# Two places for working buffers: the last 14 of 48 stand 64 bytes further on, and the operands that meet the weights take the others

## The chip, the cores and the metric

The kernel runs on one core of one Trainium2 chip. The metric is device time in microseconds, the time of one launch; the kernel was timed in three runs. One further execution was taken with the hardware profiler, and all rows below come from that one.

## The reference

The reference is a decoder trunk of two layers on 256 tokens of width 1024, all in float32. A layer has four sub-layers, each with its own RMS norm and added to the residual `h`:

```python
for l in range(DEPTH):
    h = h + 0.5 * swiglu_ffn(rms_norm(h, norm_g[l, 0]), ffn_w_in[l, 0], ffn_w_out[l, 0])
    u = rms_norm(h, norm_g[l, 1])
    z = u @ mix_w_in[l]
    ...
    y_a = rwkv7_time_mix(z_a, ...)
    y_b = retention_mix(z_b, positions, b_gn[l])
    ...
    merged = gate_a * (y_a @ w_branch_a[l]) + gate_b * (y_b @ w_branch_b[l])
    h = h + merged @ mix_w_out[l]
    h = h + memory_cross_attn(rms_norm(h, norm_g[l, 2]), mem, mem_norm[l],
                              cross_w_q[l], cross_w_kv[l], cross_w_o[l])
    h = h + 0.5 * swiglu_ffn(rms_norm(h, norm_g[l, 3]), ffn_w_in[l, 1], ffn_w_out[l, 1])
return rms_norm(h, final_norm)
```

The FFN's hidden width is 2816. The mix has an RWKV-7 branch (8 heads of 64) and a retention branch (8 heads, keys of 64, values of 128); the cross attention has 4 heads of 256 over 256 memory tokens.

## The kernel before, in words

The residual is kept transposed (`hT`, feature by token). Every large product is computed as three products of fp32r operands: each operand is split into a high and a low part, and high·high, high·low and low·high are added up in PSUM (`mm3`, which calls `mm` three times). In the profile a product reads "output<-moving,stationary 128\*128 128x256": the stationary operand is 128 by 128, the moving one 128 by 256. In the FFN `uh`/`ul` (the normed input) move and `wh`/`wl` (the weights) are loaded; in the cross attention the scores `xs` have `kT` moving and `qT` loaded, the outputs `xo` have `pT` moving and `xv` loaded, and neither operand is a weight there.

Weights come by DMA on SyncE's queue in pieces of 512 KB into five `raw` buffers; ScalarE makes the high part (`wh`, line 244), VectorE the low part (`wl`, line 245). Each has seven buffers.

Everything else that a stage needs lies in an arena of 49 buffers of 128 partitions by 2 KB (`Slots`, `s.ar`). A tile takes the buffer at the head of a queue of free ones and gives it back to the queue's end. The tiles that share a buffer are tied in order by the framework: who writes the new one waits for the last reader of the old one. Between the weights' pools and the arena stands a tile `pad` of 64 bytes (`PAD = 16` floats), and the pool `up` with `uh` and `ul` comes behind it too. The weight buffers and the arena's buffers are all multiples of 128 bytes long, so `uh`, `ul` and every arena buffer begin 64 bytes away from the 128-byte grid on which `wh` and `wl` begin. In the cross attention's `xs` and `xo` products both operands come from the arena.

The order of TensorE's instructions is written out by an event loop at build time (`Em`): tasks with a priority and a due time in a rough model of TensorE's time. The order on ScalarE, VectorE, GpSimd and SyncE is left to the framework's scheduler, which looks at dependences, at the buffers' reuse among them, and at a priority.

The names that come up below: `S` (line 1149, `mask_evac`) is the evacuation with a mask of the scores of the RWKV-7 branch from PSUM, which the next scores and the chain of that branch need. `yb<-O` (line 1483) normalises the outputs of retention with `brn`, a power that GpSimd computes (line 268) from `bss` (lines 1010 and 1480); `yb<-yb,bg` (line 1495) multiplies by the gate `bg` (lines 1438, 1440). `yaT` is the transposed output of the RWKV-7 branch, `ybT` that of retention, `mT` the merged one. `up`, `uph`, `upl` are the small up-projections of the RWKV-7 branch and their split parts. `rb`, `diagh`, `diagl`, `rx` and `sq` belong to the RMS norms. GpSimd also runs a solver of small triangular systems (`tm`, `xs`, `us`, lines 1188 and 1193).

Of the kernel before, what the change touches and what calls it, by code (L numbers as in the profile page):

```python
# [10 lines left out]
F32 = mybir.dt.float32  # L11
# [5 lines left out]
P = 128  # L17
# [55 lines left out]
class Event:  # L73
    def __init__(s):
        s.t = math.inf
# [40 lines left out]


class Slots:
    def __init__(s, pool, n, prefix, shape):
        s.pool, s.prefix, s.shape = pool, prefix, shape  # L120
        s.free_ = deque(range(n))
        s.used = {}
        s.low = n
        s.names = {}

    def alloc(s, name, dtype=F32, shape=None):
        assert s.free_, (s.prefix, "exhausted", sorted(x[1] for x in s.used.values()))
        i = s.free_.popleft()
        s.low = min(s.low, len(s.free_))
        t = s.pool.tile(list(shape or s.shape), dtype, name=name, tag=f"{s.prefix}{i}")  # L130
        s.used[id(t)] = (i, name, t)
        return t
# [7 lines left out]
class Weights:  # L140
# [10 lines left out]
    def next(s, key):  # L151
        assert s.seq[s.taken][0] == key, (s.seq[s.taken][0], key)
        s.fill()
        t = s.tiles.pop(s.taken)
        s.taken += 1
        return t
# [6 lines left out]
class K:  # L163
    NW = 7
    NRAW = 5
    NA = 49
    T_XG = 57000.0

    def __init__(s, ctx, tc, A):
        s.tc, s.nc, s.A = tc, tc.nc, A  # L170
        nc = s.nc
        ep = ctx.enter_context
        s.em = Em()
        s.pows = []
        s.const = ep(tc.tile_pool(name="const", bufs=1))
        s.rawp = ep(tc.tile_pool(name="raw", bufs=s.NRAW))
        s.wp = ep(tc.tile_pool(name="wp", bufs=s.NW))
        s.sm = ep(tc.tile_pool(name="sm", bufs=2))
        pad = ep(tc.tile_pool(name="pad", bufs=1))
        s.up = ep(tc.tile_pool(name="up", bufs=1))  # L180
        pad.tile([P, PAD], F32, name="pad")
        s.dram = ep(tc.tile_pool(name="dram", bufs=1, space=bass.MemoryType.DRAM))
        s.ar = Slots(ep(tc.tile_pool(name="ar", bufs=1)), s.NA, "a", (P, 512))
        s.ps = Slots(ep(tc.tile_pool(name="ps", bufs=1, space=bass.MemoryType.PSUM)), 8, "p", (P, 512))
        s.W = Weights(s, s.NW)
        s.setup()
        c = s.const
        s.hT = c.tile([P, 8, 256], F32, name="hT")
        s.gcol = c.tile([P, 112], F32, name="gcol")
        nc.scalar.dma_start(s.gcol, A["gcol"])  # L190
        nc.sync.dma_start(s.hT[:, 0:2, :], A["xT"][:, 0:2, :])
        s.ident = c.tile([P, P], F32, name="ident")
        nc.gpsimd.dma_start(s.ident, A["ident"])
        s.cols = c.tile([P, 8], F32, name="cols")
        nc.gpsimd.dma_start(s.cols, A["cols"])
        s.nhalf = c.tile([P, 8], F32, name="nhalf")
        nc.gpsimd.memset(s.nhalf, -0.5)
        s.ones = c.tile([P, P], F32, name="ones")
        nc.gpsimd.memset(s.ones, 1.0)
        s.onesr = c.tile([P, P], F32R, name="onesr")  # L200
        nc.gpsimd.tensor_copy(s.onesr, s.ones)
        s.cumr = c.tile([P, P], F32R, name="cumr")
        s.masks = c.tile([P, 2, P], I32, name="masks")
        s.gam = c.tile([P, 2, 2, 8], F32, name="gam")
        s.rot = [c.tile([P, 64], F32, name=f"rot{t}") for t in range(2)]
        s.S0 = c.tile([P, 4, P], F32, name="S0")
# [1566 lines left out]
```

## Time and profile before

| | us |
|---|---|
| median of 3 runs | 1493.65 |
| lowest and highest of the 3 | 1493.39, 1495.62 |
| the profiled execution's own time | 1494.51 |
| its span in the trace | 1492.7 |
| TensorE busy | 1471.5 |
| VectorE busy | 1062.8 |
| ScalarE busy | 761.4 |
| GpSimd busy | 153.6 |
| DMA moved | 270.54 MB |

The span runs from the first to the last instruction of the trace. The mean granted TensorE clock of the profiled execution is 0.993 of full speed. [...] Idle time in brackets is the time in which an engine waited, with the instruction that released it.

### The profile page before, as it was taken

The page shows a single profiled execution, that of the slowest core. Times are in us where ns is not written, and L with a number is a line of the kernel's source. Part 1 is how long each engine was busy: PE and PEld are TensorE (multiplying, and loading weights), DVE is VectorE, ACT ScalarE, POOL GpSimd, SP SyncE. Part 2 cuts the span into 40 slices and gives each one's busy share as a digit, 9 for nine tenths or more (in the row PEclk, how much of TensorE's full clock was granted, in tenths as well). Part 3 has the DMA queues.
Part 4 walks back from the last instruction along what each step waited for, and adds up shares of the span by engine and source line. Part 5 has one row for each costly group of instructions (what it writes and reads, how often), then busy time and mean ns, then how long its engine had stood idle before and what let it go on. Part 6 is the DMA issues. An engine that isn't in the chain of part 4 may idle for free.

```text
span 1492.7 us, 28682 instructions
## 1 busy us (share of the span) xinstructions
PE 1471.5 (99%) x11776; PEld 1400.1 (94%) x11776; DVE 1062.8 (71%) x1472; ACT 761.4 (51%) x1048; POOL 153.6 (10%) x231
## 2 busy tenths in 40 slices
PE   9999999998999999999999999999899999999998
PEld 9999988888999999999999999887799999999997
DVE  7975699977567757656685667899666567675654
ACT  7554475553445655444464445655354456554442
POOL 2210011281000000000001000204700000000000
PEclk9999999999999999999999999999989999999999
DMA  9776655535446545666577665675355455466661
GB/s 315 225 242 197 186 180 195 170 126 175 155 143 194 172 141 174 202 193 196 170 219 241 192 194 154 196 236 172 87 178 159 155 170 184 127 207 191 196 195 45
DMA packets 137818, 270.54 MB, mean 181 GB/s; under 512 B 18820, under 2 KB 29460, under 8 KB 137688
## 3 DMA queue, kind: packets, MB, share of 16 engines
q1 hardware_dynamic: 134552, 260.99, 56.2%
q0 software_dynamic: 2704, 7.15, 1.7%
q8 instruction: 92, 1.51, 0.4%
q10 hardware_dynamic: 432, 0.58, 0.1%
q14 instruction: 38, 0.31, 0.1%
HBM read 263.31 MB, written 2.23 MB: 178 GB/s over the span
## 4 chain that ended last, share of the span: by engine, by line
PE 87%; POOL 5%; DVE 4%; issue 2%; DMA 2%; SPq 0%; ACT 0%; POOLq 0%; DVEq 0%
PE z L210 25%; PE acc L210 21%; PE u L210 16%; PE g L210 16%; PE xq L210 3%; POOL tm L1188 3%; POOL xs L1193 2%; DVE wl L245 1%; PE tp L222 1%; PE Y L210 1%; PE xo L210 1%; PE xs L210 1%; PE sc L210 1%; PE SA L210 1%; PE low L210 1%
## 5 line engine op out<-in xcount | busy, mean ns | idle before, releaser
L245 DVE TENSOR_TENSOR wl<-raw,wh 128x1024 fp32r<-128x1024 f32 (+1 forms) x478 | 581.6, 1225 | 313.5 <-ACT wh L244 312.3
L244 ACT ACTIVATE wh<-raw 128x1024 fp32r<-128x1024 f32 (+1 forms) x478 | 502.0, 1056 | 504.6 <-PE z L210 150.1
L210 PE MATMUL g<-uh,wl 128*128 128x256 f32 x704 | 195.0, 277 | 0.2
L210 PE MATMUL u<-uh,wh 128*128 128x256 f32 x704 | 195.0, 277 | 0.0
L210 PE MATMUL g<-uh,wh 128*128 128x256 f32 x704 | 194.8, 277 | 0.0
L210 PE MATMUL g<-ul,wh 128*128 128x256 f32 x704 | 194.8, 277 | 0.0
L210 PE MATMUL u<-ul,wh 128*128 128x256 f32 x704 | 194.7, 277 | 0.0
L210 PE MATMUL u<-uh,wl 128*128 128x256 f32 x704 | 194.7, 277 | 0.0
L210 PE MATMUL acc<-ah,wh 128*128 128x256 f32 x528 | 145.8, 276 | 0.0
L210 PE MATMUL acc<-ah,wl 128*128 128x256 f32 x528 | 145.7, 276 | 0.0
L210 PE MATMUL acc<-al,wh 128*128 128x256 f32 x528 | 145.7, 276 | 0.0
L210 PEld LDWEIGHTS g<-uh,wl 128*128 128x128 f32 x704 | 132.2, 188 | 0.6 <-DVE wl L245 0.6
L210 PEld LDWEIGHTS g<-uh,wh 128*128 128x128 f32 x704 | 132.4, 188 | 0.2
L210 PEld LDWEIGHTS g<-ul,wh 128*128 128x128 f32 x704 | 132.2, 188 | 0.2
L210 PEld LDWEIGHTS u<-uh,wl 128*128 128x128 f32 x704 | 132.3, 188 | 0.0
L210 PEld LDWEIGHTS u<-uh,wh 128*128 128x128 f32 x704 | 132.2, 188 | 0.0
L210 PEld LDWEIGHTS u<-ul,wh 128*128 128x128 f32 x704 | 132.2, 188 | 0.0
L210 PE MATMUL z<-wh,uh 128*128 128x512 f32 (+1 forms) x320 | 125.3, 391 | 0.0
L210 PE MATMUL z<-wh,ul 128*128 128x512 f32 (+1 forms) x320 | 122.4, 383 | 0.7 <-DVE ul L436 0.7
L210 PE MATMUL z<-wl,uh 128*128 128x512 f32 (+1 forms) x320 | 121.5, 380 | 0.0
L210 PEld LDWEIGHTS acc<-ah,wh 128*128 128x128 f32 x528 | 99.1, 188 | 0.0
L210 PEld LDWEIGHTS acc<-al,wh 128*128 128x128 f32 x528 | 99.1, 188 | 0.0
(409 smaller groups left out, 3305.3 us busy)
## 6 DMA issues: line engine op xcount, KB each, us to landing
raw<-in_ffn_w_in SPq DMA_DIRECT2D x174, 512.0 KB, 4.5
raw<-in_mix_w_in SPq DMA_DIRECT2D x108, 512.0 KB, 4.4
raw<-in_ffn_w_out SPq DMA_DIRECT2D x88, 512.0 KB, 4.2
raw<-in_cross_w_kv SPq DMA_DIRECT2D x32, 512.0 KB, 3.7
raw<-in_w_branch_b SPq DMA_DIRECT2D x16, 512.0 KB, 3.6
raw<-in_mix_w_out SPq DMA_DIRECT2D x16, 512.0 KB, 3.4
raw<-in_cross_w_q SPq DMA_DIRECT2D x16, 512.0 KB, 3.8
raw<-in_cross_w_o SPq DMA_DIRECT2D x16, 512.0 KB, 4.2
```

The source lines that it names most:

```text
L210: s.nc.tensor.matmul(out, l, r, start=start, stop=stop)
L222: s.nc.tensor.transpose(out, src, s.ident)
L244: s.nc.scalar.activation(hi, src, AF.Copy)
L245: s.nc.vector.tensor_tensor(lo, src, hi.bitcast(F32), ALU.subtract)
L1188: i = nc.gpsimd.tensor_tensor(tm[:, 0:nr, 0:w], xc, row, ALU.mult)
L1193: nc.gpsimd.tensor_tensor(xs[:, 0:nr, k + 1:32], xs[:, 0:nr, k + 1:32], tm[:, 0:nr, 0:w], ALU.add)
```

## The change

The arena has 48 buffers in place of 49. All are now allocated at the start in one go, 34 of them, then a tile `space` of 64 bytes, then the last 14. The last 14 therefore begin on the 128-byte grid on which `wh` and `wl` begin, and the first 34 stay 64 bytes away from it. A tile whose name is in `BY_W` (the operands that are multiplied with weights, and `qT`, `pT`, `diag`) takes the first free buffer of the first part in the queue; any other tile takes the first free buffer of the last part; where that part has none, the head of the queue. `kT`, `xv` and all work that isn't an operand are among the others.

```diff
--- before.py
+++ after.py
@@ -116,16 +116,25 @@
 
 
 class Slots:
-    def __init__(s, pool, n, prefix, shape):
+
+
+    def __init__(s, pool, n, prefix, shape, nb=0, names=()):
         s.pool, s.prefix, s.shape = pool, prefix, shape
+        if nb:
+            for i in range(n):
+                if i == n - nb:
+                    pool.tile([P, 16], F32, name="space", tag="space")
+                pool.tile(list(shape), F32, name=f"{prefix}{i}", tag=f"{prefix}{i}")
         s.free_ = deque(range(n))
+        s.na, s.names = n - nb, names
         s.used = {}
         s.low = n
-        s.names = {}
 
     def alloc(s, name, dtype=F32, shape=None):
         assert s.free_, (s.prefix, "exhausted", sorted(x[1] for x in s.used.values()))
-        i = s.free_.popleft()
+        first = name in s.names
+        i = next((i for i in s.free_ if (i < s.na) == first), s.free_[0])
+        s.free_.remove(i)
         s.low = min(s.low, len(s.free_))
         t = s.pool.tile(list(shape or s.shape), dtype, name=name, tag=f"{s.prefix}{i}")
         s.used[id(t)] = (i, name, t)
@@ -163,7 +172,9 @@
 class K:
     NW = 7
     NRAW = 5
-    NA = 49
+    NA, NB = 48, 14
+
+    BY_W = {n + x for n in ("a", "mT", "yaT", "ybT", "mem", "oT", "qT", "pT", "lt", "tw", "diag", "k") for x in "hl"}
     T_XG = 57000.0
 
     def __init__(s, ctx, tc, A):
@@ -180,7 +191,7 @@
         s.up = ep(tc.tile_pool(name="up", bufs=1))
         pad.tile([P, PAD], F32, name="pad")
         s.dram = ep(tc.tile_pool(name="dram", bufs=1, space=bass.MemoryType.DRAM))
-        s.ar = Slots(ep(tc.tile_pool(name="ar", bufs=1)), s.NA, "a", (P, 512))
+        s.ar = Slots(ep(tc.tile_pool(name="ar", bufs=1)), s.NA, "a", (P, 512), s.NB, s.BY_W)
         s.ps = Slots(ep(tc.tile_pool(name="ps", bufs=1, space=bass.MemoryType.PSUM)), 8, "p", (P, 512))
         s.W = Weights(s, s.NW)
         s.setup()
```

TensorE executes the same products in the same order. The data of `uh`, `ul`, `wh`, `wl` stay where they were. Which buffer a tile gets changes almost everywhere, and with it which earlier tile it has to wait for, so that the scheduler puts some instructions of the other engines elsewhere. Two places follow. The number behind a name tells tiles of one name apart, and lines and numbers of the changed kernel are higher by 9 to 11 and by about 49.

VectorE in the mix of layer 0, around the four normalisations `yb<-O` (layer 1 has the same). Before:

```order
L1480 TENSOR_SCALAR bss_3897<-bss_3897 128x4
L1480 TENSOR_SCALAR bss_3910<-bss_3910 128x4
L1495 TENSOR_TENSOR yb_3878<-yb_3878,bg_3791 128x512
L1483 TENSOR_TENSOR yb_3895<-O_3886,brn_3900 128x512
L1483 TENSOR_TENSOR yb_3908<-O_3903,brn_3913 128x512
L1010 TENSOR_REDUCE bss_3927<-yb_3925 128x4
L245 TENSOR_TENSOR wl_3967<-raw_3965,wh_3966 128x1024
L1480 TENSOR_SCALAR bss_3927<-bss_3927 128x4
L1495 TENSOR_TENSOR yb_3895<-yb_3895,bg_3795 128x512
L1483 TENSOR_TENSOR yb_3925<-O_3916,brn_3930 128x512
```

Now:

```order
L1491 TENSOR_SCALAR bss_3946<-bss_3946 128x4
L1021 TENSOR_REDUCE bss_3959<-yb_3957 128x4
L1494 TENSOR_TENSOR yb_3944<-O_3935,brn_3949 128x512
L1491 TENSOR_SCALAR bss_3959<-bss_3959 128x4
L1021 TENSOR_REDUCE bss_3976<-yb_3974 128x4
L1494 TENSOR_TENSOR yb_3957<-O_3952,brn_3962 128x512
L1491 TENSOR_SCALAR bss_3976<-bss_3976 128x4
L1506 TENSOR_TENSOR yb_3927<-yb_3927,bg_3840 128x512
L1494 TENSOR_TENSOR yb_3974<-O_3965,brn_3979 128x512
L256 TENSOR_TENSOR wl_4016<-raw_4014,wh_4015 128x1024
```

The weight split that stood between the third and the fourth `yb<-O` (wl_3967) and the product of the second `yb` with its gate stand behind the fourth now, and the `bss` scalar that the fourth needs stands directly behind the third.

VectorE directly behind, down to the first masked evacuation `S` of this place. Before, behind yb_3925:

```order
L245 TENSOR_TENSOR wl_3989<-raw_3987,wh_3988 128x1024
L1438 SCALAR_TENSOR_TENSOR bg_3993<-bg_3993,z_3799 128x512
L1438 SCALAR_TENSOR_TENSOR bg_3997<-bg_3997,z_3800 128x512
L1440 SCALAR_TENSOR_TENSOR bg_3993<-bg_3993,rhf_2623,gn_3650 128x512
L1440 SCALAR_TENSOR_TENSOR bg_3997<-bg_3997,rhf_2623,gn_3650 128x512
L245 TENSOR_TENSOR wl_4035<-raw_4033,wh_4034 128x1024
L1495 TENSOR_TENSOR yb_3908<-yb_3908,bg_3993 128x512
L1495 TENSOR_TENSOR yb_3925<-yb_3925,bg_3997 128x512
L245 TENSOR_TENSOR wl_4065<-raw_4063,wh_4064 128x1024
L245 TENSOR_TENSOR wl_4125<-raw_4123,wh_4124 128x1024
L1149 TENSOR_TENSOR S_4103<-sc_4093,masks_97 128x512
```

Now, behind wl_4016:

```order
L1449 SCALAR_TENSOR_TENSOR bg_4042<-bg_4042,z_3848 128x512
L256 TENSOR_TENSOR wl_4038<-raw_4036,wh_4037 128x1024
L1451 SCALAR_TENSOR_TENSOR bg_4042<-bg_4042,rhf_2672,gn_3699 128x512
L1449 SCALAR_TENSOR_TENSOR bg_4046<-bg_4046,z_3849 128x512
L1506 TENSOR_TENSOR yb_3944<-yb_3944,bg_3844 128x512
L1451 SCALAR_TENSOR_TENSOR bg_4046<-bg_4046,rhf_2672,gn_3699 128x512
L256 TENSOR_TENSOR wl_4084<-raw_4082,wh_4083 128x1024
L1506 TENSOR_TENSOR yb_3957<-yb_3957,bg_4042 128x512
L1506 TENSOR_TENSOR yb_3974<-yb_3974,bg_4046 128x512
L256 TENSOR_TENSOR wl_4114<-raw_4112,wh_4113 128x1024
L256 TENSOR_TENSOR wl_4174<-raw_4172,wh_4173 128x1024
L1160 TENSOR_TENSOR S_4152<-sc_4142,masks_146 128x512
```

Between the fourth `yb<-O` and `S` stood four weight splits, four `bg` and two `yb` products before; now there are five, four and three.

VectorE at the head of the mix of layer 1, where the last `ul` parts of the norm are made. Before:

```order
L691 TENSOR_TENSOR hT_82<-hT_82,dh_11128 128x512
L436 SCALAR_TENSOR_TENSOR ul_11002<-hT_82,gcol_83,uh_11001 128x256
L245 TENSOR_TENSOR wl_11147<-raw_11145,wh_11146 128x1024
L436 SCALAR_TENSOR_TENSOR ul_11002<-hT_82,gcol_83,uh_11001 128x256 x2
L446 TENSOR_TENSOR sq_11034<-sq_11034,sq_11135 128x512
L245 TENSOR_TENSOR wl_11153<-raw_11151,wh_11152 128x1024
L449 TENSOR_TENSOR sq_11034<-sq_11034 128x256
```

Now:

```order
L702 TENSOR_TENSOR hT_131<-hT_131,dh_11177 128x512
L447 SCALAR_TENSOR_TENSOR ul_11051<-hT_131,gcol_132,uh_11050 128x256
L256 TENSOR_TENSOR upl_11301<-wup_11290,uph_11298 65x512
L447 SCALAR_TENSOR_TENSOR ul_11051<-hT_131,gcol_132,uh_11050 128x256 x2
L457 TENSOR_TENSOR sq_11083<-sq_11083,sq_11184 128x512
L256 TENSOR_TENSOR upl_11303<-gup_11292,uph_11300 128x512
L460 TENSOR_TENSOR sq_11083<-sq_11083 128x256
```

The three splits `upl` stood some 70 rows further up, in the FFN; now they stand in the norm, and the weight split between the `ul` parts has moved behind them. In layer 0 the three splits moved into the norm too, but there a weight split still stands ahead of the last two `ul` parts.

## Rows read from the trace of the kernel before

**Rows 1.** Two lines of the profile's page: from its first part TensorE's busy time, share of the span and instructions, and from its fourth part the chain that ended last, by engine.

```profile
PE 1471.5 (99%) x11776; PEld 1400.1 (94%) x11776; DVE 1062.8 (71%) x1472; ACT 761.4 (51%) x1048; POOL 153.6 (10%) x231
...
PE 87%; POOL 5%; DVE 4%; issue 2%; DMA 2%; SPq 0%; ACT 0%; POOLq 0%; DVEq 0%
```

**Rows 2.** The list of waits of TensorE over the whole span: who waited for whom, us in total, times, longest.

```profile
PE sc L210 <- DVE S L1149: 11.0, 2, 5.5
```

**Rows 3.** TensorE's instructions in order of time around the second pair of `xo` heads of layer 0: start in us, its modelled duration in us, then engine, line, operation, output<-moving,stationary and count.

```profile
540.62 0.28 PE L210 MATMUL acc<-oTh,wh 128*128 128x256 f32 x1
...
543.68 0.28 PE L210 MATMUL xo<-pTh,xvh 128*128 128x256 f32 x1
...
546.56 0.28 PE L210 MATMUL acc<-oTh,wh 128*128 128x256 f32 x1
...
579.77 0.27 PE L210 MATMUL rb<-ones,sq 128*128 128x128 f32 x1
```

**Rows 4.** Groups of TensorE's instructions, busy us and modelled mean ns of one: first from 540.61 to 543.60 us, then from 546.55 to 579.70 us. Each row stands for one of three products with the same count, mean and operands (hi and lo parts exchanged), give or take one at the edge of the window.

```profile
L210 PE MATMUL acc<-oTh,wh 128*128 128x256 f32 x9 | 2.5, 276 | 0.0
...
L210 PE MATMUL acc<-oTh,wh 128*128 128x256 f32 x54 | 15.2, 281 | 0.0
...
L210 PE MATMUL g<-uh,wh 128*128 128x256 f32 x32 | 9.0, 281 | 0.0
...
L210 PE MATMUL u<-uh,wh 128*128 128x256 f32 x8 | 2.2, 281 | 0.0
```

**Rows 5.** The stretch behind the second pair of `xo` heads in layer 1, its first product and what ends it, in order of time (columns as in rows 3).

```profile
1283.59 0.28 PE L210 MATMUL acc<-oTh,wh 128*128 128x256 f32 x1
...
1316.81 0.27 PE L210 MATMUL rb<-ones,sq 128*128 128x128 f32 x1
```

**Rows 6.** Groups of TensorE's instructions (columns as in rows 4): the first pair of `xo` heads from 530.97 to 533.80 us, and the `xs` products from 511.06 to 513.93 us.

```profile
L210 PE MATMUL xo<-pTh,xvh 128*128 128x256 f32 x8 | 2.3, 283 | 0.0
...
L210 PE MATMUL xs<-kTh,qTh 128*128 128x256 f32 x8 | 2.3, 283 | 0.0
```

**Rows 7.** The products of `yaT` from 465.88 to 474 us as a group (columns as in rows 4), and in order of time the first of the stretch behind them and what ends it (columns as in rows 3).

```profile
L210 PE MATMUL z<-yaTl,wh 128*128 128x256 f32 x24 | 6.6, 276 | 0.0
...
473.94 0.28 PE L210 MATMUL acc<-mTh,wh 128*128 128x256 f32 x1
...
502.50 0.27 PE L210 MATMUL rb<-ones,sq 128*128 128x128 f32 x1
```

**Rows 8.** VectorE in order of time in layer 0, ahead of the evacuation of the masked scores `S` (start, duration of all of the row, line, operation, names, shapes, count, and in brackets idle time before it and its releaser).

```profile
333.76 1.31 DVE L245 TENSOR_TENSOR wl<-raw,wh 128x1024 fp32r<-128x1024 f32 x1
...
335.07 0.68 DVE L1495 TENSOR_TENSOR yb<-yb,bg 128x512 f32<-128x512 f32 x1
336.66 0.69 DVE L1483 TENSOR_TENSOR yb<-O,brn 128x512 f32<-128x512 f32 x1 [0.91 <-POOL brn L268]
337.26 1.22 DVE L245 TENSOR_TENSOR wl<-raw,wh 128x1024 fp32r<-128x1024 f32 x1
338.40 1.28 DVE L1438 SCALAR_TENSOR_TENSOR bg<-bg,z 128x512 f32<-128x512 f32 x2
339.59 1.41 DVE L1440 SCALAR_TENSOR_TENSOR bg<-bg,rhf,gn 128x512 f32<-128x512 f32 x2
340.92 1.22 DVE L245 TENSOR_TENSOR wl<-raw,wh 128x1024 fp32r<-128x1024 f32 x1
342.05 1.29 DVE L1495 TENSOR_TENSOR yb<-yb,bg 128x512 f32<-128x512 f32 x2
343.26 2.35 DVE L245 TENSOR_TENSOR wl<-raw,wh 128x1024 fp32r<-128x1024 f32 x2
345.53 1.28 DVE L1149 TENSOR_TENSOR S<-sc,masks 128x512 int32<-128x512 int32 x2
```

**Rows 9.** GpSimd in the same stretch: the three powers `brn` (columns as in rows 8).

```profile
330.53 2.00 POOL L268 TENSOR_TENSOR brn<-bss,nhalf 128x4 f32<-128x4 f32 x2
...
335.23 1.39 POOL L268 TENSOR_TENSOR brn<-bss,nhalf 128x4 f32<-128x4 f32 x1 [1.24 <-DVE bss L1480]
```

**Rows 10.** TensorE's first product behind the long wait of layer 0, in order of time, and busy time, granted clock (PEclk), DMA share and GB/s in two stretches of each layer: the long wait and what follows it until the clock is back.

```profile
346.27 0.58 PE L210 MATMUL sc<-mh,kh 64*128 64x256 f32 x1 [5.46 <-DVE S L1149]
...
340.65:346.27 5.62, 0.17 (x3) 0.01 (x1) 5.62 (x8) 0.00 (x0) 0.93 (x2) 0.98 0.46 115
346.27:352.85 6.58, 6.56 (x32) 6.04 (x33) 5.88 (x9) 3.76 (x6) 0.00 (x0) 0.50 0.63 168
...
1077.40:1083.08 5.68, 0.18 (x2) 0.00 (x1) 5.68 (x8) 0.00 (x0) 0.99 (x2) 0.72 0.50 122
1083.08:1090.13 7.05, 7.03 (x35) 6.51 (x36) 6.35 (x9) 3.76 (x6) 0.00 (x0) 0.50 0.64 179
```

**Rows 11.** Layer 1 in order of time: the evacuation of `S` on VectorE, and at the head of the mix the last two `ul` tiles with the weight split ahead of them on VectorE and the product on TensorE that waits for them.

```profile
929.97 1.22 DVE L245 TENSOR_TENSOR wl<-raw,wh 128x1024 fp32r<-128x1024 f32 x1
931.10 0.88 DVE L436 SCALAR_TENSOR_TENSOR ul<-hT,gcol,uh 128x256 fp32r<-128x256 f32 x2
...
931.64 0.39 PE L210 MATMUL z<-wh,ul 128*128 128x256 f32 x1 [0.36 <-DVE ul L436]
...
1082.33 1.29 DVE L1149 TENSOR_TENSOR S<-sc,masks 128x512 int32<-128x512 int32 x2
```

**Rows 12.** The instructions that write one of the split decay weights `upl`: count, duration in ns (min/median/max), first and last start.

```profile
L245 DVE TENSOR_TENSOR upl<-wup,uph x2: 680/680/681, 101.3 to 827.0; 65x512 fp32r<-65x512 f32 x2
```

## The prediction

> **What bounds the kernel now.** I read the page first: TensorE is busy in 99% of the span and holds 87% of the chain that ended last [rows 1]. So nothing on another engine is worth time by itself; only two things are: how fast TensorE's products follow each other, and the few places at which TensorE waits. The list of waits has one large entry, the scores `sc` of the RWKV-7 branch that wait for VectorE's masked evacuation `S`: 11.0 us in two waits, one in each layer [rows 2].
>
> For the pace I read TensorE in order of time and take starts, since the durations are modelled. Ahead of the second pair of `xo` heads 27 products of `oT` follow each other in 543.68 - 540.62 = 3.06 us, 113.3 ns each. The 24 `xo` products take 546.56 - 543.68 = 2.88 us, 120.0 ns each. Behind them the very same kind of `oT` products and then the FFN's, 3 x (54 + 32 + 8) = 282, take 579.77 - 546.56 = 33.21 us, 117.8 ns each [rows 3, 4]. In the groups the same three paces show as mean durations of 276, 283 and 281 ns [rows 4, 6]. Layer 1 repeats it: 1316.81 - 1283.59 = 33.22 us [rows 5]. The products with 120 ns (`xs`, `xo`) are those in which the moving operand and the next stationary one both come from the arena, and so both begin 64 bytes off the 128-byte grid; where one is a weight tile and the other not, 113.3 ns is what they reach. And the slow pace outlives its cause: the 282 products have operands on different places and still run at 117.8.
>
> **The change, part by part.** *Pace of the scores and outputs.* Following the buffers' queue through the program, all `xs` and the second `xo` pair of each layer now have their operands on different places, and about half of the products of the first `xo` pair. The second `xo` pair goes from 120.0 to 113.3 ns: 24 x 6.7 = 0.16 us. The two `xs` groups (48 products) gain between 2.2 and 6.7 ns each, 0.1 to 0.3 us; I take 0.2. The first `xo` pair gains half of 0.16, 0.08. Largest is what follows: if the second `xo` pair no longer sets the slow pace, the 282 products run at 113.3: 282 x 4.5 = 1.25 us. Together 1.7 us a layer, 3.4 in both. The bounds: least, `xs` and `xo` only come down to 117.8 and the run behind stays, 84 x 2.2 = 0.2 a layer, 0.4 in all; at most, 3.8.
>
> *A new pair on one place.* The second half of `yaTl` finds the first part empty and takes buffers of the last part, on the grid of the weights: 16 of the 72 products of that stretch in each layer now move from the place from which the next weight is loaded. They run at 276 ns now [rows 7]. One in three or less on the same place may cost nothing, or up to 16 x 6.7 = 0.11 us; I take 0.05. The upper end is that it sets the slow pace for what follows: 72 products and the (502.50 - 473.94)/0.1133 = 252 behind them [rows 7], 324 x 4.5 = 1.46 us, with the 0.11 together 1.57 a layer. I take the small value, since in the stretch before `xo` the pace returned to 113.3 by itself [rows 3].
>
> *The evacuation S comes later.* This is the other side. In layer 0 the fourth `yb<-O` starts at 336.66 and `S` at 345.53, 8.87 us later, and VectorE never idles between them [rows 8]; TensorE stands until 346.27 [rows 10]. In the new order one weight split (338.40 - 337.26 = 1.14 us) and one `yb` product ((343.26 - 342.05)/2 = 0.60) stand in this piece that stood ahead of the fourth `yb<-O` before, at 333.76 and 335.07 [rows 8]. So 10.61 us from there. Does the fourth `yb<-O` come earlier in return? It waits for GpSimd's power `brn`, at 335.23 before, behind a wait of 1.24 us for `bss` [rows 9]. In the new order `bss` comes as soon as the third `yb<-O` is done, but the third power now waits for the second `yb<-O` (0.69 us) where it ran directly behind the second power until 332.53 [rows 9], and solver steps stand between it and the fourth. The fourth can gain between 0 and 1.24 us; I take 0.4. Then `S` starts 1.74 - 0.4 = 1.34 us later, bounds 0.5 and 1.74. TensorE has nothing else to do there, so this is paid in full, and in layer 1, whose `S` starts at 1082.33 with the same rows ahead [rows 11], once more: +2.7 us, bounds 1.0 to 3.5. The weight splits that stand there are not themselves awaited; what is queued behind them is `S` alone.
>
> [...]
>
> *Head of the mix.* In layer 1 TensorE waits 0.36 us for the last two `ul`, ahead of which VectorE splits a weight for 931.10 - 929.97 = 1.13 us [rows 11]. A split `upl` of 0.68 us stands there now [rows 12]: 0.4 us less, bounds 0 and 0.5. In layer 0 the weight split stays ahead of them: 0. The other two `upl` are covered by TensorE's products of `z`, for which the weights lie ready; without that cover each would cost its 0.68 us.
>
> *The rest.* All other moves are on engines with idle time and have buffers ready ahead of them; one arena buffer less makes a few loads wait for an earlier reader, far ahead of their use. I take 0, with 1 us to either side.
>
> The sum: -3.4 + 0.1 + 2.7 - 0.4 = -1.0 us on the profiled execution's 1494.51, which is 1493.5. The median of the runs lies 0.86 us below that execution, so 1492.6.
>
> [...] The rows say that two operands on one place cost up to 6.7 ns a product [rows 3]. [...]
>
> **The rivals.** [...]
>
> *Second, slower: the new pair sets the slow pace.* `yaTl` puts its stretch and the 252 products behind it at 117.8 (1.57 a layer), and the 282 behind `xo` stay slow, since whatever perturbs the rhythm there starts them: -0.4 + 3.1 + 2.7 - 0.4 = +5.0, 1498.7. It decides for slower as soon as more than two thirds of these 3.1 us are there. For it: the slow pace outlived its cause once [rows 4]. Against: the pairs are isolated ones.
>
> *Third, place has no effect.* Then only the order counts: 2.7 - 0.4 = +2.3, 1495.95. For it: the paces differ by place in two kinds of product only.
>
> **How the numbers follow.** A measurement of this kernel can tell about 0.2%, 3.0 us, from no change. The forecast gets 0.40, the first rival 0.23, the second 0.17, the third 0.10; 0.10 is left for a late weight or buffer that I don't see, or a gain of that kind. Faster by more than 3.0 us: most of the first rival, a little of the forecast and of the rest, 0.27. Slower by more: most of the second, a part of the third and of the rest, 0.26. Within: 0.47. The range, 1488 to 1499, reaches from 2 us below the first rival to the second.
>
> **What would show it.** In the profile after, the mean durations of `xs` and of the second `xo` should fall from 283 to 276 or at least to 281, and the stretch behind `xo` from 281 to 276 [rows 4, 6]; if `xo` falls and the stretch doesn't, the step from the pair to the run is wrong. `z<-yaTl` should stay at 276 [rows 7]. The wait for `S` should grow from 11.0 to about 13.7 us [rows 2]; if it is below 11.5, the working of the order is wrong, and the time should then be near 1490. A new entry in the list of waits of more than 1 us would make the whole sum wrong.

## The result: slower by 1.0%, and the profile after

The changed kernel takes 1508.69 us (median of 4 runs, 1507.14 to 1510.23) against 1493.95 us before (4 runs, 1493.39 to 1495.62): a ratio of 1.0099, 95% interval 1.0088 to 1.0111, or +14.7 us. The forecast was 1492.6, the range ended at 1499. The profiled execution took 1507.14 us (span 1505.3), before 1494.51 (span 1492.7); these 12.6 us are what the two traces can explain.

The page of the changed kernel first, as in [rows 1]:

```profile
PE 1473.0 (98%) x11776; PEld 1399.7 (93%) x11776; DVE 1064.3 (71%) x1472; ACT 762.8 (51%) x1048; POOL 157.4 (10%) x231
...
PE 85%; POOL 5%; DVE 4%; DMA 2%; issue 2%; ACT 1%; SPq 0%; POOLq 0%; DVEq 0%; ACTq 0%
```

TensorE's busy time is nearly the same (1473.0 against 1471.5), and the rest of the span has grown: the time was lost by waiting. The list of waits of TensorE, us in total, times, longest, answers to [rows 2]:

```profile
PE sc L221 <- DVE S L1160: 11.0, 2, 5.5
PE z L221 <- ACT tm L951: 8.5, 2, 5.0
PE z L221 <- DVE bg L1449: 2.6, 2, 1.3
...
PE tp L233 <- ACT zl L904: 0.5, 1, 0.5
PE z L221 <- DVE ul L447: 0.4, 1, 0.4
```

`S` is unchanged at 11.0 us. Two entries are new: `z` waits for ScalarE's `tm` (8.5 us, once in each layer) and for VectorE's `bg` (2.6 us, once in each layer); a smaller one is `zl`.

Since TensorE executes the same instructions in the same order, the start of each can be compared between the two traces. The lag is how much later an instruction starts than before. This is how it builds up:

| stretch | lag at its end, us | change |
|---|---|---|
| up to the low-rank part of layer 0 | 0.15 | +0.15 |
| wait for `tm`, and the half clock behind it | 7.75 | +7.6 |
| up to the retention part | 7.2 | -0.5 |
| waits for `bg` and `S` | 8.8 | +1.6 |
| up to the second `xo` pair | 8.55 | -0.2 |
| the stretch behind it | 7.35 | -1.2 |
| head of the mix, layer 1 | 8.0 | +0.65 |
| wait for `tm`, and the half clock | 13.15 | +5.2 |
| up to the retention part | 12.35 | -0.8 |
| waits for `bg` and `S` | 13.9 | +1.6 |
| half clock behind it ends earlier | 12.7 | -1.2 |
| `yaT`, `xs`, `xo` and the stretch behind them | 11.4 | -1.3 |
| second FFN of layer 1 | 12.6 | +1.2 |

The two waits for `tm` with their half clock (0.50 granted, shown below) are 12.8 us, as much as the whole lag at the end; all the rest adds up to about zero (-0.2). ScalarE in order of time in layer 0, in the changed kernel (start, duration of all of the row, line, operation, names, shapes, count, and in brackets idle time and its releaser):

```profile
221.53 0.60 ACT L948 ACTIVATE tw<-low 128x512 f32<-128x512 f32 x1
223.40 0.63 ACT L1035 ACTIVATE sq<-kk 128x512 f32<-128x512 f32 x1 [1.26 <-DVE zk L1009]
...
224.93 0.59 ACT L948 ACTIVATE tw<-low 128x512 f32<-128x512 f32 x1
...
226.41 0.64 ACT L1035 ACTIVATE sq<-kk 128x512 f32<-128x512 f32 x1
...
228.59 1.21 ACT L951 ACTIVATE tm<-low 64x512 f32<-64x512 f32 x2
```

And ScalarE in the kernel before, the same instructions:

```profile
219.33 0.60 ACT L937 ACTIVATE tw<-low 128x512 f32<-128x512 f32 x1 [0.48 <-PE low L210]
219.95 0.60 ACT L940 ACTIVATE tm<-low 64x512 f32<-64x512 f32 x1
...
223.20 0.59 ACT L940 ACTIVATE tm<-low 64x512 f32<-64x512 f32 x1
```

`tm` is the tanh of the decay's low-rank product `low`, written in two halves of 64 partitions from two PSUM tiles. Before, each stood directly behind `tw`, at 219.95 and 223.20; now both stand at 228.59, behind both `sq`. Until both halves are read, two PSUM tiles of `low` are not free, and the next `z`, which needs a PSUM tile, waits for `tm`. TensorE in order of time, with all three waits of layer 0:

```profile
229.24 0.80 PE L221 MATMUL z<-wh,uh 128*128 128x512 f32 x1 [4.96 <-ACT tm L951]
...
348.56 0.39 PE L221 MATMUL z<-uh,wh 128*128 128x256 f32 x1 [1.29 <-DVE bg L1449]
...
355.04 0.58 PE L221 MATMUL sc<-mh,kh 64*128 64x256 f32 x1 [5.50 <-DVE S L1160]
```

And the busy time of each engine, the granted clock (PEclk), DMA share and GB/s, in the wait for `tm` and behind it, in both layers:

```profile
223.88:229.24 5.36, 0.40 (x3) 0.01 (x1) 5.03 (x11) 5.31 (x11) 1.43 (x1) 0.85 0.63 194
229.24:234.40 5.16, 5.16 (x12) 4.14 (x13) 3.98 (x7) 1.13 (x2) 2.23 (x2) 0.50 0.33 101
968.28:972.26 3.98, 0.40 (x3) 0.01 (x1) 3.42 (x8) 3.93 (x8) 1.66 (x1) 0.94 0.26 96
972.26:974.98 2.72, 2.72 (x6) 2.15 (x7) 1.98 (x4) 1.13 (x2) 1.83 (x2) 0.50 0.33 102
```

In the wait TensorE is busy for 0.40 of 5.36 us, and behind it the granted clock is 0.50 for 5.16 us in layer 0 and for 2.72 us in layer 1. There a 512-wide product takes 427 ns from start to start instead of 230, which costs 2.5 and 1.3 us more.

Next, VectorE from the fourth `yb<-O` to `S`, the first and the last row of the stretch that [rows 8] show of before:

```profile
343.69 0.69 DVE L1494 TENSOR_TENSOR yb<-O,brn 128x512 f32<-128x512 f32 x1 [1.53 <-POOL brn L279]
...
354.29 1.29 DVE L1160 TENSOR_TENSOR S<-sc,masks 128x512 int32<-128x512 int32 x2
```

From one to the other it is 10.60 us; the prediction had worked out 10.61.

Last, the pace: groups of TensorE's instructions (busy us, modelled mean ns of one), the second `xo` pair and the stretch behind it in layer 0, the products of `yaT`, and a stretch of the second FFN of layer 1. They answer to [rows 4, 6, 7]:

```profile
L221 PE MATMUL z<-yaTl,wh 128*128 128x256 f32 x23 | 6.4, 279 | 0.0
...
L221 PE MATMUL xo<-pTh,xvh 128*128 128x256 f32 x8 | 2.2, 276 | 0.0
...
L221 PE MATMUL acc<-oTh,wh 128*128 128x256 f32 x54 | 14.9, 276 | 0.0
...
L221 PE MATMUL g<-uh,wh 128*128 128x256 f32 x32 | 8.8, 276 | 0.0
...
L221 PE MATMUL u<-uh,wl 128*128 128x256 f32 x46 | 12.9, 281 | 0.0
```

`xo` has come from 283 to 276 ns (from start to start 24 products take 555.00 - 552.28 = 2.72 us, 113.3 ns each, against 120.0 before, so that the modelled durations overlap) and the stretch behind it from 281 to 276, as forecast. `yaTl` has gone from 276 to 279, and a stretch of the FFN of layer 1, at 276 ns before, runs at 281 now.

### The profile page after: what moved, and what is told of

Its sections match the earlier page's. It is cut to its first block, busy times and chain, and to the rows that moved or that the text cites. A ratio compares the mean times of both kernels' runs of the same rounds, so it can differ in the third digit from the quotient of the medians.

```text
span 1505.3 us, 28701 instructions
## 1 busy us (share of the span) xinstructions
PE 1473.0 (98%) x11776; PEld 1399.7 (93%) x11776; DVE 1064.3 (71%) x1472; ACT 762.8 (51%) x1048; POOL 157.4 (10%) x231
## 4 chain that ended last, share of the span: by engine, by line
PE 85%; POOL 5%; DVE 4%; DMA 2%; issue 2%; ACT 1%; SPq 0%; POOLq 0%; DVEq 0%; ACTq 0%
PE z L221 23%; PE acc L221 21%; PE u L221 16%; PE g L221 15%; PE xq L221 3%; POOL tm L1199 3%; POOL xs L1204 2%; DVE wl L256 1%; PE Y L221 1%; PE tp L233 1%; DMA us<-ug 1%; PE xs L221 1%; PE xo L221 1%; PE sc L221 1%; PE SA L221 1%
```

## The experiments

Theory A, formed from this profile: the time was lost by the order, not by the place. A part of 14 buffers for everything that isn't an operand of weights runs down to one or two free ones, so that one tile after another takes the buffer just given back. Following the queue through the program, in layer 0 the tile `tm` stands in the buffer that held `za`, then `zs`, then the first `sq` of the keys, then the second, all within the mix; each has to wait for the last reader of the one before. In the kernel before the five have buffers of their own that were given back long before. Theory B: the place itself does the harm.

The names of that chain: `za` is an input of the low-rank part; `zs` is the copy of the keys moved on by one token, brought by DMA, from which VectorE makes `zk` and `kk`; ScalarE squares `kk` into `sq`, and VectorE sums `sq` up as `kss`.

**The change without the second place.** All orders as in the changed kernel.

```diff
-                if i == n - nb:
-                    pool.tile([P, 16], F32, name="space", tag="space")
```

> The changed kernel without the 64-byte tile between the two parts: the same names, parts and instruction orders on every engine, but all arena buffers 64 bytes off the grid of the weights again. Theory A (the 14.7 us come from the order: buffers of a short queue that tm, the masked evacuation and others have to wait for; the place itself only helps): the pace gain goes and nothing else, so 1508.7 plus about 2.9 us, 1511 to 1512; the wait of z for ACT tm stays at 8.5 us in two, the stretch behind the second xo pair has a mean of 281 ns again. Theory B (the place does the harm, say a slower access of the engines on the last part): back near 1494, and the wait for tm gone.

Measured 1508.85 us; ratio to before 1.0098 (1.0084 to 1.0111). Its waits of TensorE, and the stretch behind `xo`:

```profile
...
PE z L219 <- ACT tm L949: 8.1, 2, 4.2
PE z L219 <- DVE bg L1447: 2.7, 2, 1.4
```

```profile
L219 PE MATMUL xo<-pTl,xvh 128*128 128x256 f32 x8 | 2.3, 283 | 0.0
...
L219 PE MATMUL acc<-oTh,wh 128*128 128x256 f32 x54 | 15.2, 281 | 0.0
```

and of the second FFN of layer 1:

```profile
L219 PE MATMUL u<-uh,wh 128*128 128x256 f32 x45 | 12.4, 276 | 0.0
```

Theory B falls: without the second place the time is the same, and the waits are nearly the same. The pace does go back to 283 and 281 ns, but the +2.9 us expected from it isn't there: the stretch in the FFN of layer 1 that ran at 281 in the changed kernel runs at 276 here, which gives 1.2 us back; the profiled span is longer by 1.4 us only, and the medians differ by 0.2.

**One buffer less, and nothing else.**

```diff
-    NA = 49
+    NA = 48
```

> The kernel before with 48 instead of 49 buffers, one queue, no parts, no space. Theory A1 (one buffer less alone moves the yb products and a weight split behind the fourth yb evacuation, and so delays S; the tm wait is not from it): +2.8 us, 1496.5, a new wait of z or sc of about 1.3 us in each layer, no wait for ACT tm. Theory A2 (the lost buffer is also what makes tm late): near 1508. Theory B: 1494.

Measured 1495.49 us; ratio 1.0006 (0.9997 to 1.0015).

```profile
PE sc L210 <- DVE S L1149: 11.0, 2, 5.5
PE z L210 <- DVE bg L1438: 1.8, 2, 1.0
```

The wait for `bg` (1.8 us) is here in the old kernel with one queue, and VectorE's order between the fourth `yb<-O` and `S` is that of the changed kernel. So the lost buffer, given up for 64 bytes of space, is by itself enough for that order. I had expected a wait of 1.3 us in each layer and a time 2.8 us longer; the wait is 0.9. A difference of 1.5 us is at the edge of what the runs tell; the wait in the trace says it more clearly.

**Only `tm` in the buffer of `sq`, in the kernel before.**

```diff
-        i = s.free_.popleft()
+        i = s.free_[-2 if name == "tm" and shape is None else 0]
+        s.free_.remove(i)
```

> The kernel before with one edit: the tile tm of the low-rank part takes the buffer that the second squared-key tile sq has just given back, as it does in the changed kernel, instead of the head of the queue; both of its writes then wait on VectorE's sum kss of that sq. Theory A: this alone brings the stall: z waits for ACT tm about 4 to 5 us in each layer, with the granted clock at 0.5 for some us behind it, so plus 10 to 13 us, 1504 to 1507. Rival (tm was late in the changed kernel for another reason, such as a later kk chain or VectorE's more work there): 1494 to 1496.

Measured 1494.53 us; ratio 1.0002 (0.9994 to 1.0011). My expectation was wrong: `tm` moved to 223.25 us and the wait for it isn't in the list. The scheduler put the sum `kss` that `tm` waits for early, and ScalarE was done before the PSUM tiles were wanted. One late link isn't enough.

**The last links: both `sq` and `tm` in one buffer, and then with `zs` late as well.** Both in the kernel before. In the first, only `sq` and `tm` take the buffer given back last; in the second (shown), every `zs` too, and that of the keys then waits for the readers of the low-rank inputs.

```diff
-        i = s.free_.popleft()
+        late = shape is None and name in ("zs", "sq", "tm")
+        i = s.free_[-2 if name == "tm" and late else -1 if late else 0]
+        s.free_.remove(i)
```

> As the run before, but only sq, sq and tm share one buffer; zs takes the queue's head. It tells which link counts. If the two sq and tm are enough: 1500 to 1507 as well. If the late zs is what counts, since then the chain starts some us earlier and ends before its PSUM tile is wanted: 1494 to 1496.

> The kernel before, one queue and 49 buffers, with one edit: the tiles zs, sq of the keys and tm take the buffer given back last, instead of the one at the queue's head, so that sq, sq and tm share one buffer one after the other and zs waits for the low-rank inputs, as in the changed kernel. Theory A: this alone, without any second place, brings the wait for ACT tm of some us in each layer: 1502 to 1507. Rival (the chain of buffers doesn't matter by itself): 1494 to 1496.

Measured: `sq` and `tm` alone 1495.82 us, ratio 1.0010 (1.0001 to 1.0019); with `zs` 1518.66 us, ratio 1.0161 (1.0148 to 1.0174). ScalarE with `sq` and `tm` alone:

```profile
218.73 0.62 ACT L1026 ACTIVATE sq<-kk 128x512 f32<-128x512 f32 x1
...
221.95 0.63 ACT L1026 ACTIVATE sq<-kk 128x512 f32<-128x512 f32 x1
...
224.10 1.21 ACT L942 ACTIVATE tm<-low 64x512 f32<-64x512 f32 x2
```

ScalarE with `zs` late as well, and below the longest wait of TensorE there:

```profile
226.40 0.62 ACT L1026 ACTIVATE sq<-kk 128x512 f32<-128x512 f32 x1
228.22 0.63 ACT L1026 ACTIVATE sq<-kk 128x512 f32<-128x512 f32 x1 [1.20 <-DVE kss L1012]
232.84 1.21 ACT L942 ACTIVATE tm<-low 64x512 f32<-64x512 f32 x2 [3.99 <-DVE kss L1012]
```

```profile
PE z L212 <- ACT tm L942: 18.0, 2, 9.4
```

This is the stall of the changed kernel, made in the old one without any second place, and larger (18.0 us of waiting). The chain needs both ends: `zs` late, so that the first `sq` starts at 226.40 instead of 218.73, and then `sq`, `kss`, `sq`, `kss`, `tm` one behind the other, since ScalarE waits for VectorE at each link (1.20 and 3.99 us). Not all of the 7.7 us is the buffer's own wait: `zs` is mixed 3.1 us later (217.59 against 214.51), and for the rest VectorE's new order has put other work ahead of `kk`. With the early start the same links end at 224.10, and TensorE has no wait for `tm`; the 1.9 us by which the median is above the kernel before are at the edge of what the runs tell, and no wait in the trace accounts for them.

**A larger last part in the changed kernel.**

```diff
-    NA, NB = 48, 14
+    NA, NB = 48, 26
```

> The changed kernel with 26 buffers in the last part instead of 14, same names and same rule of choice: the last part doesn't run dry in the low-rank part, so tm, zs and the sq of the keys no longer share one buffer. Theory A (a part of 14 runs down to one or two free buffers, so one tile after another takes the buffer just given back and they run one after the other: za, zs, sq, sq, tm): no wait for ACT tm, 1508.7 less about 12 us, 1495 to 1498 (the S delay of 48 buffers stays, and more operands of yaT and mem now share a place with the weights). Rival (the tm wait is from the choice by name or the order that it makes, whatever the part's size): still 1505 or more.

Measured 1499.19 us; ratio 1.0031 (1.0019 to 1.0043).

```profile
PE sc L221 <- DVE S L1160: 8.6, 3, 4.9
PE sc L221 <- DVE rS L1160: 1.9, 2, 1.1
PE R L221 <- DVE S L1160: 1.6, 2, 1.2
```

```profile
L221 PE MATMUL acc<-oTh,wh 128*128 128x256 f32 x64 | 18.0, 281 | 0.0
...
L221 PE MATMUL xo<-pTh,xvh 128*128 128x256 f32 x8 | 2.2, 281 | 0.0
```

The wait for `tm` is gone, and the time is 9.5 us less. It isn't all of it. TensorE now waits for VectorE's `S` and `rS` seven times, 12.1 us, in place of two waits of 11.0. And with only 22 buffers in the first part, all of `yaT` and part of `mem` now lie on the place of the weights. The second `xo` pair and the products of `oT` on both sides of it are at 281 ns, although `kT`, `xv`, `qT` and `pT` lie where they do in the changed kernel.

**The late key chain without its last link.** In the changed kernel `tm`, `tw`, `ta` and `g` take the first part; `za`, `zs` and both `sq` still share one buffer.

```diff
-... for x in "hl"}
+... for x in "hl"} | {"tm", "tw", "ta", "g"}
```

> The changed kernel with tm, tw, ta and g added to the names that take the first part. za, zs and the two sq of the keys still share one buffer one after the other, but tm and tw no longer end that chain. Theory A': the late key chain alone costs nothing on TensorE, only its last link does, tm, which holds the PSUM tile of the low-rank product: no wait for ACT tm, 1508.7 less about 12 us, 1495.5 to 1498. Rival (the late key chain itself delays ScalarE or VectorE there): 1503 or more, with another wait of z in its place.

Measured 1502.65 us; ratio 1.0062 (1.0049 to 1.0074): between the two.

```profile
...
PE z L221 <- DVE bg L1449: 2.9, 2, 1.4
PE sc L221 <- DVE yb L1494: 2.1, 2, 1.1
PE R L221 <- DVE zv L1136: 1.2, 2, 0.9
...
PE sc L221 <- DVE bss L1491: 1.1, 2, 0.5
```

There is no wait for `tm` any more, 6 us less. But four waits of 7.3 us in total stand in the list, of which the changed kernel had only `bg` with 2.6; theory A' had no such price. That they come from the late key chain isn't shown: they lie some 60 us and more behind it, and the kernel with 26 buffers, in which the tiles of the chain have buffers of their own, waits at the product `R` as well.

**The change with all 49 buffers.** The 14 stand ahead of the pad, on the grid of the weights, so that no space is needed.

```diff
-    NA, NB = 48, 14
+    NA, NB = 49, 14
...
+        last = ep(tc.tile_pool(name="last", bufs=1))
         pad = ep(tc.tile_pool(name="pad", bufs=1))
```

> The change with all 49 buffers (35 and 14; the 14 stand ahead of the pad, on the grid of the weights, so that no space tile is needed). The chain za, zs, sq, sq, tm in one buffer is the same as in the changed kernel. Theory A: the buffer lost costs only the later S, 1.3 us a layer; the wait for tm stays: 1505.5 to 1508. Rival (with one buffer more the last part's neighbours come free in time): below 1500.

Measured 1506.52 us; ratio 1.0086 (1.0071 to 1.0102).

```profile
PE z L217 <- ACT tm L947: 8.8, 2, 4.6
PE z L217 <- DVE bg L1445: 2.2, 2, 1.4
```

The wait for `tm` stays, as expected. But the wait for `bg`, which I had put down to the lost buffer, stays as well: from the fourth `yb<-O` to `S` VectorE takes 10.00 us here, against 8.87 before and 10.60 in the changed kernel. The two parts alone make most of that order, too. The buffer is worth 2.2 us in the medians and 0.8 in the traces' spans.

**Places without the short queue.** Two versions with 49 buffers, the last part ahead of the pad as above, in which only a few tiles prefer the last part, operands of weights the first, and every other tile takes the head of the one queue, as before. In the first the last part has 8 buffers and is preferred by `qT` and `pT`, in the second 16 and by `kT` and `xv`:

```diff
-        first = name in s.names
-        i = next((i for i in s.free_ if (i < s.na) == first), s.free_[0])
+        want = name in s.names if name in s.names or name[:2] in ("kT", "xv") else None
+        i = next((i for i in s.free_ if want is None or (i < s.na) == want), s.free_[0])
```

> All 49 buffers; the last part has 8 of them and stands ahead of the pad, so no space tile is needed; only qT and pT prefer the last part, the operands of weights prefer the others, every other tile takes the head of the queue as before. xo has no pair on one place, xs about a third of its pairs, yaTl 8 of 36 triples. Instruction orders nearly as before. Theory A: the pace gain without the stalls: -2.5 to -3.4 us, 1490.5 to 1491.5, mean of the stretch behind the second xo pair 276 ns, waits as before (S 11.0, no tm). Rival (the pace behind xo is set by something else than xo's places): 1493.5 to 1494.5.

> 49 buffers, the last part has 16 and stands ahead of the pad; kT and xv prefer the last part, operands of weights the other, every other tile takes the head of the queue. xs free of pairs on one place, xo but for 8, and in xs and xo the moving and the loaded operand lie on the same sides as in the changed kernel; yaTl has 32 pairs. Theory C (the slow stretch behind xo begins where the places of the moving and of the loaded operand swap sides between xo and the weights, or a pair on one place): stretch behind the second xo pair at 276 ns as in the changed kernel, waits as in the kernel before: 1490.5 to 1492. Rival (the pace falls and rises by chance of the entry): 1493 to 1495.

Measured: `qT` and `pT` 1493.29 us, ratio 0.9996 (0.9987 to 1.0004); `kT` and `xv` 1491.61 us, ratio 0.9984 (0.9976 to 0.9993), faster than both kernels. The second `xo` pair and the stretch behind it, first with `qT` and `pT` on the last part:

```profile
L217 PE MATMUL xo<-pTl,xvh 128*128 128x256 f32 x8 | 2.3, 281 | 0.0
...
L217 PE MATMUL acc<-oTh,wh 128*128 128x256 f32 x54 | 15.2, 281 | 0.0
```

the first `xo` pair of the same kernel,

```profile
L217 PE MATMUL xo<-pTh,xvh 128*128 128x256 f32 x8 | 2.2, 277 | 0.0
```

and with `kT` and `xv` on it, with that kernel's longest wait:

```profile
L217 PE MATMUL xo<-pTh,xvh 128*128 128x256 f32 x8 | 2.2, 276 | 0.0
...
L217 PE MATMUL acc<-oTh,wh 128*128 128x256 f32 x54 | 14.9, 276 | 0.0
```

```profile
PE sc L217 <- DVE S L1156: 10.9, 2, 5.5
```

In both, no `xo` product in this pair has its two operands on one place. With `qT` and `pT` the pace is 281 all the same, in `xo` and behind it; with `kT` and `xv` it is 276. What differs by theory C is the side: in the first the moving operand of `xo` lies on the weights' grid and the loaded one off it, the other way round than in the products ahead and behind, so that at both borders one product moves from the place from which the next one is loaded. This pair fits theory C, a slow pace that is set at a single border and lasts. But the first pair with `qT` and `pT`, whose operands lie on the same sides, runs at 277. And with 26 buffers, on the sides of `kT` and `xv`, the pair runs at 281, a pace that is there ahead of it already and goes on. What sets the pace, and why it lasts, no run here shows. The trace of `kT` and `xv` is 3.8 us shorter than that of the kernel before: the pace gains 3.7 us there, `yaT` and a stretch of the FFN give 1.7 back, and the half clock behind the waits for `S` ends earlier by 1.9 (mean granted clock 0.994 against 0.993). So the 2.3 us of the medians are about what the pace leaves.

## Why the prediction was wrong

The step that failed is "**The rest**": "All other moves are on engines with idle time and have buffers ready ahead of them; one arena buffer less makes a few loads wait for an earlier reader, far ahead of their use. I take 0, with 1 us to either side." There it was +12.8 us, the two waits for `tm` with the half clock behind them. The prediction's own sign, a new entry of more than 1 us in the list of waits, came up twice (`tm` 8.5, `bg` 2.6). I had followed which buffers the operands get, and the new order on VectorE, but not which earlier tile each buffer of the last part had held and when that was last read. A part of 14 buffers that serves everything else recycles them within a few instructions, and a chain of tiles in one buffer ties ScalarE and VectorE together link by link. The order of ScalarE shows it too: `tm<-low` stands behind both `sq<-kk` in the changed kernel. The chain in the old kernel brings the wait (18.0 us, +24.7 in the time), the larger part and the freed last link remove it (-9.5 and -6): this shows that it is the cause. That the last link alone brings nothing, nor the last links without the late `zs`, shows that it is the chain and not one wait.

That all the rest came to about zero, close to the forecast of -1.0, is in part luck: terms that I didn't have (the FFN +1.2, the head of the mix +1.1, the shorter dips -1.6) cancel.

By its other steps:

- *Pace of `xs`, `xo` and the stretch behind.* Forecast -3.4 us; the lag falls there by 1.4 us in layer 0 and by 1.7 in layer 1, 3.1 in all. Right in size and place: each of the two stretches behind `xo` gives the 1.25 us forecast. Taking the 64 bytes away puts 276 back to 283 and 281 with all orders the same, so the third rival, that place has no effect, is ruled out.
- *What the pace gave back.* A stretch of the FFN of layer 1 that no edit touches went from 276 to 281 ns, +1.2 us. I had no term for it. It is slow in the changed kernel and fast in the one without the space; it is slow, too, with 26 buffers, with the freed last link, with all 49 buffers, and with `kT` and `xv`, and fast with `qT` and `pT`. The cause is open.
- *The new pair, `yaTl`.* Forecast 0.05 a layer; 279 to 281 ns instead of 276 in some 70 products is 0.3 a layer, and the stretch behind it stayed at the fast pace. The second rival's knock-on didn't happen.
- *The evacuation S.* Forecast +2.7 us. The waits for `bg` and `S` cost 1.6 us more in each layer; 0.3 and 0.7 of that had been saved just ahead, at a `sc` that waited for the fourth `yb<-O` before, so 2.1 are left. The working of the order was right (10.60 us against 10.61), but the wait shows elsewhere: `S` still has 11.0 us and `bg`, of which a `z` ahead waits for the PSUM tile, has 2.6. Either half of the change brings a wait for `bg` by itself: 48 buffers in one queue (1.8) and 49 in two parts (2.2).
- *Head of the mix.* The 0.4 us for `ul` in layer 1 were saved (a lag of 7.4 fell to 6.9). Behind it +1.1 us came: the three `upl` and the weight splits stand ahead of `rst`, which `zl` needs, and the transposes waited 0.5 us for `zl`. I had said that the cover of `z` hides them; there it doesn't.
- *The clock.* Behind the waits for `S`, which were as long as before, the granted clock was at 0.50 for 5.75 us in layer 0 and 4.50 in layer 1, against 6.58 and 7.05 before [rows 10]. That saved 0.4 and 1.2 us; why it was shorter isn't shown. Two more dips, behind `tm`, belong to the step that failed.

## What to carry to other kernels

A pool of buffers that serves by place must still be long enough in each part: before splitting a queue, list for each tile which tile held its buffer before and when that is last read, and look at the instructions that hold PSUM. Give a place only to the few tiles that need it and let all others take the oldest free buffer; here that turned +14.7 us into -2.3. And look for the bytes of a shift where there are some already (a pad) before giving up a buffer.

## What the runs showed of the hardware

A shift of 64 bytes of one part of the buffers, with all orders the same, took the second `xo` pair, in which the moving operand and the operand loaded next had lain on one place, from 283 to 276 ns in the modelled duration; from start to start a product of this pair takes 120 ns in the kernel before, where it is at 283 as well, and 113 in the changed one. There is a third pace, 281 ns or 118 from start to start, which in the kernel before holds over some 280 products whose moving and loaded operands lie on different places. It can begin with the 24 `xo` products ahead (281 with `qT` and `pT` on the last part, 276 with `kT` and `xv`), but the sides of their operands don't settle it: the first pair with `qT` and `pT` runs at 277, and with 26 buffers, where the operands lie as with `kT` and `xv`, a pace of 281 goes on through them. The two stalls of TensorE for `tm`, of 5.36 and 3.98 us, were followed by a granted clock of 0.50 for 5.16 and 2.72 us, in which a 512-wide product took 427 ns in place of 230; that cost 2.5 and 1.3 us more, nearly a half and a third of the stall.
